# One of layer 1's two modulation sums goes from VectorE, ScalarE and GpSimd to TensorE, and from the first out projection into the layer 0 mixers

## The chip, the cores and the metric

The kernel runs on one core of one Trainium2 chip. The metric is device time in microseconds (us) of one execution; lower is better. An engine's instructions run in the order of its queue: PE is TensorE (weight loads apart, as PEld), DVE is VectorE, ACT is ScalarE, POOL is GpSimd, SP is the queue that issues all the DMAs.

## The reference

Two layers of a diffusion backbone over 640 tokens (128 of context, 512 latent) of width 2048. Each layer's norm is modulated by three vectors of 2048, for each of two conditions (`c_ctx` and `c`):

```
def adaln(x, cond, norm_w, w_ada, b_ada):
    mod = jax.nn.silu(cond) @ w_ada + b_ada
    shift, scale, gate = jnp.split(mod, 3, axis=-1)
    return rmsnorm(x, norm_w) * (1 + scale) + shift, gate
...
    for li in range(DEPTH):
        hc, gate_c = adaln(xc, cc, norm_w[li], w_ada[li], b_ada[li])
        hl, gate_l = adaln(xl, cl, norm_w[li], w_ada[li], b_ada[li])
        ...  # even layer: DeltaNet and windowed attention; odd layer: GLA and neighbourhood attention
        xc = xc + gate_c * (oc @ w_out)
        xl = xl + gate_l * (ol @ w_out)
```

So layer 1's shift and scale are each a product of two condition vectors with a 2048 x 2048 part of `w_ada[1]` (16.8 MB in float32). They depend on no token. They are needed when layer 1's input is normed, which is after the first out projection (`@ w_out` of layer 0).

## The kernel before

Activations stand transposed, 128 features by 640 tokens a tile (16 tiles). A projection is done in units: one unit makes 128 output features of all tokens, in two halves of 320 tokens, each an accumulator `acc` in PSUM (the pool `pacc` holds three). Weights come in quarters of a unit (`weights`, L1040 on): a DMA into `w_st`, ACT rounds it to `w_hi`, DVE subtracts to get `w_lo` (L1050); each of `w_st`, `w_hi`, `w_lo` has three buffers. For each of the 16 feature tiles and each half there are three matmuls (`hh,w_hi`, `hl,w_hi`, `hh,w_lo`), so a unit has 96 matmuls and a quarter 24.

The program has these stages: a start with layer 0's norm; the layer 0 mixers, where `run` lays the heads' streams and, as filling, the units of the input projection one after another on PE; the first out projection (`out_proj`); the layer 1 mixers; the second out projection. In the mixers of layer 0 the order of PE is that of the recording (`keep_in_program_order`), and so is it in `out_proj`; the other engines' order is set by a scheduler that works on modelled times.

There are two ways to make a modulation vector.

- `ada` gives it to TensorE. A step loads 128 x 512 of `w_ada` into a slot of `adv` (L1269), four matmuls of 32 columns each, on four column groups of the array, multiply it with the conditions (`ada_ps`; the profile counts two instructions for each, as they are float32), and DVE adds the PSUM tile to `adv` (L1286, or L1284 for the first of a chunk). 16 steps make a chunk of 512 outputs, 64 steps a vector. After a chunk `ada_out` transposes it and writes `mod`. Layer 0's gate is made this way in the layer 0 mixers, with one slot; its pacing is `yield 7`.
- `ada_vec` sums on vector engines. A step loads 128 x 512 of `w_ada` (L1305) and for each condition multiplies it with 128 scalars and adds it to a running 128 x 512 sum: on DVE in one instruction (L1319; L1317 for the first of a chunk), or on ACT (L1322, into `scale_t`) with the addition on POOL (L1324). After 16 steps PE sums over the partitions (`adv_ps`), and `ada_out` writes `mod`.

Before the change both vectors of layer 1 are made in `out_proj` of layer 0 with `ada_vec`: the scale (tile `scale`) with one condition on DVE and one on ACT and POOL, the shift (tile `vec`) with both on DVE. `side` advances both together. `out_proj` takes a step of this filling after every six of its main steps, and a main step is three matmuls; so 18 steps (16 and two more, a chunk) go with 324 matmuls, and the 72 steps with 1296.

When a unit is done, `residual` does three instructions on DVE (L1518: `x` from `acc`, gate and the old `x`; only then is `acc` free), a DMA writes `x` out, ACT squares it, POOL adds the square to `n_acc` (L1462), and when the scale of this tile is there POOL multiplies `x` with it (`scaled`, L1422, two instructions). Before, tiles wait for their chunk of the scale.

Of the kernel before, what the change touches and what calls it, by code (L numbers as in the profile page):

```python
# [1201 lines left out]
def run(g, main, *streams):  # L1202


    live = [[s, None, g.now] for s in streams]
    while live:
        for e in live:
            if e[2] <= g.now if e[1] is None else e[1]():
                try:
                    y = next(e[0])  # L1210
                    e[1], e[2] = (y, 0) if callable(y) else (None, g.now + (y or 0))
                except StopIteration:
                    live.remove(e)
                break
        else:
            if not main.step():
                nn = min([e[2] for e in live if e[1] is None] + [main.when()])
                assert nn < INF
                g.now = nn
# [147 lines left out]
def vec_store(pool, n, nt, width=512, name="vec"):  # L1367

    t = pool.tile([128, 2 + n, width], F32, name=name)
    return t[:, 0:2], [t[:, 2 + i] for i in range(n)], partial(pool.tile, [128, width], F32, name=f"{name}_t", bufs=nt)  # L1370


def ada_store(pool, n, k, width=512):

    w = width // 4
    t = pool.tile([128, w + n * k * width], F32, name="adv")
    return t[:, 0:w], [t[:, w + j * k * width:w + (j + 1) * k * width] for j in range(n)]
# [169 lines left out]
def body(nc, tc, I, O):  # L1547
    off = [(k, v.shape[1]) for k, v in const_table().items()]
    with ExitStack() as es:
        g = G()  # L1550
# [4 lines left out]
        pool = lambda e, n, b=1, **k: e.enter_context(tc.tile_pool(name=n, bufs=b, **k))  # L1555
# [34 lines left out]
        with ExitStack() as e1:  # L1590
            px = pool(e1, "px0")
# [12 lines left out]
            store = ada_store(px, 3, 4)  # L1604
# [45 lines left out]
        with ExitStack() as e1:  # L1650
            g.pt = pool(e1, "pt", 3)
            g.pz = pool(e1, "pz")
            g.pat = pool(e1, "pat")
            g.pss = pool(e1, "pss", 2, space=PSUM)
            g.psg = pool(e1, "psg1", 2, space=PSUM)
            a_setup(g, e1)
            b_setup(g, e1)
            g.spare = 8
            main = Main(g, hh, hl, zip(EARLY, parts), slabs[-1][0])
            get = lambda n, prio, now=False: main.ask(W[n], prio, now, n)  # L1660
            prepped, inverted, values, gates, queried, bgates, st = {}, {}, {}, {}, {}, {}, dict(b=0, joined=-1, scanned=-1, ready={}, gates=False)

            tri = g.pe.tile([128, T], F32, name="g_tri", tag="a_o1", bufs=2)
            nc.sync.dma_start(tri[:, 0:512], I["a_tab"])

            def first():
                ps = yield from get(32, -1)
                gs = g.pe.tile([128, T], F32, name="gs", tag="a_o0", bufs=2)
                for i in range(2):
                    nc.scalar.copy(gs[0:64, i * 320:i * 320 + 320], ps[i][0:64])  # L1670
                yield LAT["drain"]
                yield from a_gates(g, gs, tri)
                st["gates"] = True

            def prep():
                for h in range(8):
                    yield lambda: st["joined"] >= h - 2
                    k = a_conv(g, h, 1, (yield from get(8 + h, 0.5)))
                    yield lambda: st["scanned"] >= h - 2
                    q = a_conv(g, h, 0, (yield from get(h, 0.5)))  # L1680
                    yield LAT["conv"]
                    yield lambda: st["gates"]
                    prepped[h] = yield from a_prep(g, h, q, k)
                    st["ready"][h] = g.now

            def value():
                for h in range(8):
                    yield lambda: st["joined"] >= h - 1 and h in st["ready"]
                    values[h] = a_conv(g, h, 2, (yield from get(16 + h, 1)))
                    yield LAT["conv"]  # L1690
                    values[h, 1] = True

            def zgate():
                for h in range(8):
                    yield lambda: st["scanned"] >= h - 1 and len(st["ready"]) >= h + 1
                    gates[h] = silu2(g, (yield from get(24 + h, 2)), g.pz, "zs_a")

            def inverses():
                for h in range(8):
                    yield lambda: st["joined"] >= h - 1 and h in prepped  # L1700
                    yield max(0, st["ready"][h] + LAT["inv"] - LAT["invld"] - g.now)
                    inverted[h] = a_inverted(g, h, *prepped[h]["inv"]), g.now

            def scans():
                for h in range(8):
                    yield lambda: (h, 1) in values and h in inverted
                    yield max(0, inverted[h][1] + LAT["invld"] - g.now)
                    prepped[h]["inv"] = inverted.pop(h)[0]
                    oT = yield from a_scan(g, prepped.pop(h), values.pop(h), gates, st)
                    g.outs.emit(h, oT)  # L1710
                    st["scanned"] = h

            def queries():
                for h in range(8):
                    yield lambda: len(st["ready"]) >= h and st["b"] >= h - 1
                    if h == 0:
                        yield from b_kv(g, 0, get(41, 3), get(43, 3))
                    queried[h] = yield from b_query(g, h, get(33 + h, 3))
                    st["q", h] = g.now

            def bgate():
                for h in range(8):
                    yield lambda: h in queried and st["b"] >= h - 1
                    bgates[h] = silu2(g, (yield from get(45 + h, 4)), g.pz, bufs=2)

            def bs():
                for h in range(8):
                    if h == 4:
                        yield from b_kv(g, 1, get(42, 0), get(44, 0))
                    yield lambda: h in queried  # L1730
                    yield max(0, st["q", h] + LAT["rope"] - g.now)
                    yield from b_head(g, h, queried[h], bgates)
                    st["b"] = h + 1

            gate = ada(g, 0, (2,), [512] * (2048 // 512), ada_store(g.pa1, 1, 1, 512), 7)
            outs = g.outs = Outs(g, main, 53, I["w_out_even"], ORDER0, 2)
            run(g, main, inverses(), scans(), first(), prep(), value(), bs(), queries(), zgate(), bgate(), gate, outs.stream())
        e0.close()

        with ExitStack() as e1:  # L1740
            px = pool(e1, "px1")
            g.pt2 = pool(e1, "pt2")
            g.psg = pool(e1, "psg2", 4, space=PSUM)
            steps = ada_vec(g, 1, 1, vec_store(px, 4, 2, name="scale"), ('dve', 'act'))
            steps = side(steps, ada_vec(g, 1, 0, vec_store(px, 4, 2), ('dve', 'dve')))
            sh = mod(g, 1, 0)

            def end(t, xs, accs):

                cs = slice(t * 320, t * 320 + 320)  # L1750
                for _ in range(2):
                    yield
                R = yield from rstd(g, px, accs, t * 320, 320, 64)
                for k in range(16):
                    h = px.tile([128, T], F32, name="h_t", tag="h_t", bufs=3)
                    times(g, h[:, cs], xs[k][:, cs], R, k % 3)
                    for c0, c1, cd in REG:
                        c0, c1 = max(c0, cs.start), min(c1, cs.stop)
                        if c0 < c1:
                            hi, lo = (x[k][:, c0:c1] for x in (outs.main.hh, outs.main.hl))  # L1760
                            nc.scalar.activation(hi, h[:, c0:c1], AF.Identity, bias=sh[:, k, cd:cd + 1])
                            nc.vector.scalar_tensor_tensor(out=lo, in0=h[:, c0:c1], scalar=sh[:, k, cd:cd + 1], in1=hi,
                                                           op0=ALU.add, op1=ALU.subtract)
                    if k % 2:
                        yield

            out_proj(g, 0, outs, px, lambda n: I["xT"][n], lambda n: x1[n], steps,
                     lambda n: g.mod[1, 1][:, n] if g.mods.get((1, 1), 0) > n else None, end)
            hs = [(outs.main.hh[k], outs.main.hl[k]) for k in range(16)]
            hh, hl = zip(*hs)  # L1770

# [201 lines left out]
```

## Time and profile before

| | us |
|---|---|
| median of 3 runs (2791.26 to 2799.9) | 2797.22 |
| the profiled execution | 2803.32 |
| its span in the profile | 2801.5 |
| PE busy (share of the span) | 2623.7 (94%) |
| DVE busy | 1650.0 (59%) |
| ACT busy | 998.2 (36%) |
| POOL busy | 800.3 (29%) |

A busy time is the time in which at least one instruction of the engine ran. Matmuls are pipelined, so a busy PE need not be at its peak. What a change in one stage is worth has to be read from that stage. The granted clock tells TensorE's share of 2.4 GHz; 0.5 is 1.2 GHz.

### The profile page before, as it was taken

The page shows a single profiled execution, that of the slowest core. Times are in us where ns is not written, and L with a number is a line of the kernel's source. Part 1 is how long each engine was busy: PE and PEld are TensorE (multiplying, and loading weights), DVE is VectorE, ACT ScalarE, POOL GpSimd, SP SyncE. Part 2 cuts the span into 40 slices and gives each one's busy share as a digit, 9 for nine tenths or more (in the row PEclk, how much of TensorE's full clock was granted, in tenths as well). Part 3 has the DMA queues.
Part 4 walks back from the last instruction along what each step waited for, and adds up shares of the span by engine and source line. Part 5 has one row for each costly group of instructions (what it writes and reads, how often), then busy time and mean ns, then how long its engine had stood idle before and what let it go on. Part 6 is the DMA issues. An engine that isn't in the chain of part 4 may idle for free.

```text
span 2801.5 us, 53986 instructions
## 1 busy us (share of the span) xinstructions
PE 2623.7 (94%) x20855; PEld 2458.3 (88%) x20855; DVE 1650.0 (59%) x3618; ACT 998.2 (36%) x2214; POOL 800.3 (29%) x946
## 2 busy tenths in 40 slices
PE   6889899999999999997979899999999999999997
PEld 5778787787878988997879799999999999999996
DVE  5765556565655664469998855454553636455225
ACT  3232342333333434353333543334324333343222
POOL 2326415053350550005554431013001201220223
PEclk9989999999999999998889999999999999999998
DMA  9933333332322222247665332232332323225334
GB/s 330 304 91 92 92 92 86 95 95 81 103 85 72 76 69 69 79 162 233 216 205 169 117 101 91 80 112 70 103 110 75 98 78 103 97 66 178 99 99 136
DMA packets 264705, 329.81 MB, mean 118 GB/s; under 512 B 76013, under 2 KB 148925, under 8 KB 264447
## 3 DMA queue, kind: packets, MB, share of 16 engines
q1 hardware_dynamic: 264447, 326.35, 36.8%
q8 instruction: 164, 2.69, 0.4%
q14 instruction: 94, 0.77, 0.1%
HBM read 294.95 MB, written 28.68 MB: 116 GB/s over the span
## 4 chain that ended last, share of the span: by engine, by line
PE 70%; DVE 10%; issue 9%; DMA 7%; POOL 2%; ACT 1%; SPq 1%; DVEq 0%; POOLq 0%; ACTq 0%
PE acc L77 55%; PE a_st L77 3%; DVE vec L1319 2%; DMA a_df<-gc_d 2%; PE at_s L77 2%; PE at_o L77 2%; DVE w_lo L1050 1%; PE ada_ps L77 1%; DVE scale L1319 1%; PE c_ops L77 1%; PE at_pt L84 1%; DMA adv<-w_ada 1%; PE c_lv L77 1%; POOL i_tmp L493 1%; POOL i_S L495 1%
## 5 line engine op out<-in xcount | busy, mean ns | idle before, releaser
L77 PE MATMUL acc<-hh,w_hi 128*128 128x320 f32 (+1 forms) x4544 | 1462.7, 323 | 53.4 <-DVE x L1518 42.5
L77 PE MATMUL acc<-hl,w_hi 128*128 128x320 f32 (+1 forms) x4544 | 1425.9, 314 | 9.1 <-DVE hl L1228 8.5
L77 PE MATMUL acc<-hh,w_lo 128*128 128x320 f32 x4480 | 1405.3, 314 | 11.5 <-DVE w_lo L1050 11.5
L77 PEld LDWEIGHTS acc<-hh,w_hi 128*128 128x128 f32 (+1 forms) x4544 | 866.2, 191 | 101.6 <-issue 73.5
L77 PEld LDWEIGHTS acc<-hl,w_hi 128*128 128x128 f32 (+1 forms) x4544 | 866.9, 191 | 14.7 <-DVE hl L1228 12.2
L77 PEld LDWEIGHTS acc<-hh,w_lo 128*128 128x128 f32 x4480 | 856.9, 191 | 14.4 <-DVE w_lo L1050 13.5
L1050 DVE TENSOR_TENSOR w_lo<-w_st,w_hi 128x512 fp32r<-128x512 f32 x561 | 435.9, 778 | 537.3 <-ACT w_hi L1048 532.0
L1048 ACT CAST w_hi<-w_st 128x512 fp32r<-128x512 f32 (+1 forms) x604 | 364.8, 604 | 835.8 <-PE acc L77 713.2
L1319 DVE SCALAR_TENSOR_TENSOR vec<-vec,cond 128x256 f32<-128x256 f32 (+1 forms) x360 | 248.8, 727 | 22.3 <-DMA vec<-w_ada 21.1
L495 POOL TENSOR_TENSOR i_S<-i_S,i_tmp 40x30 f32<-40x30 f32 (+14 forms) x240 | 144.6, 602 | 18.6
L493 POOL TENSOR_TENSOR i_tmp<-i_S 40x30 f32<-40x30 f32 (+14 forms) x240 | 136.6, 569 | 18.1
L1324 POOL TENSOR_TENSOR scale<-scale,scale_t 128x512 f32<-128x512 f32 x60 | 94.5, 1575 | 121.5 <-ACT scale_t L1322 61.7
L928 POOL TENSOR_TENSOR c_X<-c_b 128x320 f32<-128x320 f32 x56 | 46.9, 837 | 227.0 <-PE c_lv L77 199.6
L1462 POOL TENSOR_TENSOR n_acc<-n_acc,n_sq 128x640 f32<-128x640 f32 (+1 forms) x30 | 47.8, 1595 | 204.0 <-ACT n_sq L1461 204.0
L302 POOL TENSOR_TENSOR a_at<-a_df,consts 128x640 f32<-128x640 f32 x8 | 13.0, 1627 | 323.8 <-PE a_st L77 97.2
L789 POOL TENSOR_TENSOR d_bias<-d_braw,d_mask 128x256 f32<-128x256 f32 x32 | 28.5, 920 | 230.6 <-PE tm_ps L84 90.7
L77 PE MATMUL ada_ps<-adv,cond 128*32 128x128 f32 x1536 | 68.1, 299 | 25.2 <-DMA adv<-w_ada 23.6
L215 DVE SCALAR_TENSOR_TENSOR a_y<-a_pad,consts,a_y 128x644 f32<-128x644 f32 x96 | 90.1, 938 | 2.1
L77 PEld LDWEIGHTS ada_ps<-adv,cond 128*32 128x32 f32 x1536 | 39.2, 116 | 46.1 <-DVE n_acc L1462 19.6
L1322 ACT ACTIVATE scale_t<-scale,cond 128x512 f32<-128x512 f32 x60 | 43.0, 722 | 95.7 <-DMA scale<-w_ada 83.8
L1050 POOL TENSOR_TENSOR w_lo<-w_st,w_hi 128x256 fp32r<-128x256 f32 (+1 forms) x43 | 35.8, 838 | 105.2 <-ACT w_hi L1048 82.7
L593 ACT ACTIVATE at_S<-at_S,at_nm 128x384 f32<-128x384 f32 (+2 forms) x80 | 47.5, 594 | 49.9 <-DVE at_nm L591 49.6
(321 smaller groups left out, 2894.1 us busy)
## 6 DMA issues: line engine op xcount, KB each, us to landing
w_st<-w_in_odd SPq DMA_DIRECT2D x232, 256.0 KB
adv<-w_ada SPq DMA_DIRECT2D x192, 256.0 KB
w_st<-w_in_even SPq DMA_DIRECT2D x188, 256.0 KB
w_st<-w_out_even SPq DMA_DIRECT2D x72, 256.0 KB
w_st<-w_out_odd SPq DMA_DIRECT2D x72, 256.0 KB
scale<-w_ada SPq DMA_DIRECT2D x64, 256.0 KB
vec<-w_ada SPq DMA_DIRECT2D x64, 256.0 KB
vec<-w_ada SPq DMA_DIRECT2D x128, 128.0 KB
```

Of the source, the lines that this page charges most:

```text
L77: i = self.nc.tensor.matmul(out, lhsT=lhsT, rhs=rhs, **kw)
L215: nc.vector.scalar_tensor_tensor(out=y, in0=pad[:, j:j + CL], scalar=w[:, j:j + 1], in1=y, op0=ALU.mult, op1=ALU.add)
L493: E.tensor_tensor(out=t, in0=S[:, j + 1:, j].unsqueeze(2).to_broadcast([40, n, j]), in1=S[:, j, 0:j].unsqueeze(1).to_broadcast([40, n, j]) ...
L495: E.tensor_tensor(out=S[:, j + 1:, 0:j], in0=S[:, j + 1:, 0:j], in1=t, op=ALU.add)
L593: nc.scalar.activation(S[:, 0:n], S[:, 0:n], AF.Exp, bias=nm, accum_out=den[:, 0:1])
L928: nc.gpsimd.tensor_tensor(out=pv(X[0])[:, :, 1 - d], in0=bv[:, :, 1 - d], in1=bm, op=ALU.subtract)
L1048: nc.scalar.copy(hi, st)
L1050: (nc.gpsimd if g.spare >= 0 else nc.vector).tensor_tensor(out=lo, in0=st, in1=hi, op=ALU.subtract)
L1319: nc.vector.scalar_tensor_tensor(out=acc[:, c], in0=st, scalar=sc, in1=acc[:, c], op0=ALU.mult, op1=ALU.add)
L1322: nc.scalar.activation(t, st, AF.Copy, scale=sc)
L1324: nc.gpsimd.tensor_tensor(out=acc[:, c], in0=acc[:, c], in1=t, op=ALU.add)
L1462: eng.tensor_add(accs[0][:, cs], accs[0][:, cs], t[:, cs])
```

## The change

Layer 1's scale is made by `ada` in the layer 0 mixers, with a pool of its own of three slots (`pv`), from the time that two heads are prepared, paced by `yield 4`. In `out_proj` only the shift is left, as it was, both conditions on DVE. `scaled` finds the scale there from the first tile on. The pool takes its place in SBUF from the scratch that the program holds for DMAs issued by GpSimd (`dynamic_dma_scratch_size`); no DMA of this kernel is issued there.

```diff
@@ -1651,6 +1651,7 @@
             g.pat = pool(e1, "pat")
+            g.pv = pool(e1, "pv")
             g.pss = pool(e1, "pss", 2, space=PSUM)
@@ -1733,16 +1734,21 @@
             gate = ada(g, 0, (2,), [512] * (2048 // 512), ada_store(g.pa1, 1, 1, 512), 7)
+            store = ada_store(g.pv, 3, 1)
+
+            def ahead():
+
+                yield lambda: len(st["ready"]) >= 2
+                yield from ada(g, 1, (1,), [512] * 4, store, 4)
+
             outs = g.outs = Outs(g, main, 53, I["w_out_even"], ORDER0, 2)
-            run(g, main, inverses(), scans(), first(), prep(), value(), bs(), queries(), zgate(), bgate(), gate, outs.stream())
+            run(g, main, inverses(), scans(), first(), prep(), value(), bs(), queries(), zgate(), bgate(), gate, ahead(), outs.stream())
...
-            steps = ada_vec(g, 1, 1, vec_store(px, 4, 2, name="scale"), ('dve', 'act'))
-            steps = side(steps, ada_vec(g, 1, 0, vec_store(px, 4, 2), ('dve', 'dve')))
             sh = mod(g, 1, 0)
...
-            out_proj(g, 0, outs, px, lambda n: I["xT"][n], lambda n: x1[n], steps,
-                     lambda n: g.mod[1, 1][:, n] if g.mods.get((1, 1), 0) > n else None, end)
+            out_proj(g, 0, outs, px, lambda n: I["xT"][n], lambda n: x1[n],
+                     ada_vec(g, 1, 0, vec_store(px, 4, 2), ("dve", "dve")),
+                     lambda n: g.mod[1, 1][:, n], end)
@@ -1960,7 +1967,7 @@
-    nc = _bacc.Bacc("TRN2", target_bir_lowering=False, num_devices=1)
+    nc = _bacc.Bacc("TRN2", target_bir_lowering=False, num_devices=1, dynamic_dma_scratch_size=1024)
```

Counted over the whole program, this takes 64 multiply-adds and 4 copies from DVE, 64 instructions from ACT, 60 additions from POOL, and 36 small matmuls from PE in the out projection; it puts 256 matmuls (512 instructions) and 4 transposes on PE and 64 additions or copies of 128 x 128 on DVE in the mixers. The 64 loads of 256 KB go from the one stage to the other. All other instructions stay in number, and PE's matmuls of the projections in the out projection stand as they did.

The change moves rows on DVE and on PE. First DVE in the first out projection, from one weight quarter within a unit to the next unit's residual (`vec` is the sum of the shift, `scale` that of the scale, `w_lo` the low part of a weight quarter). Before:

```order
L1050 TENSOR_TENSOR w_lo<-w_st,w_hi 128x512
L1319 SCALAR_TENSOR_TENSOR scale<-scale,cond 128x512
L1319 SCALAR_TENSOR_TENSOR vec<-vec,cond 128x512 x2
L1050 TENSOR_TENSOR w_lo<-w_st,w_hi 128x512
L1319 SCALAR_TENSOR_TENSOR scale<-scale,cond 128x512
L1319 SCALAR_TENSOR_TENSOR vec<-vec,cond 128x512 x2
L1319 SCALAR_TENSOR_TENSOR scale<-scale,cond 128x512
L1050 TENSOR_TENSOR w_lo<-w_st,w_hi 128x512
L1319 SCALAR_TENSOR_TENSOR vec<-vec,cond 128x512
L1518 SCALAR_TENSOR_TENSOR x_15722<-acc,mod_3936,x_old 128x128
```

And now, at a like place in a unit:

```order
L1050 TENSOR_TENSOR w_lo<-w_st,w_hi 128x512
L1319 SCALAR_TENSOR_TENSOR vec<-vec,cond 128x512 x3
L1050 TENSOR_TENSOR w_lo<-w_st,w_hi 128x512
L1319 SCALAR_TENSOR_TENSOR vec<-vec,cond 128x512 x4
L1050 TENSOR_TENSOR w_lo<-w_st,w_hi 128x512
L1319 SCALAR_TENSOR_TENSOR vec<-vec,cond 128x512 x4
L1050 TENSOR_TENSOR w_lo<-w_st,w_hi 128x512
L1319 SCALAR_TENSOR_TENSOR vec<-vec,cond 128x512 x2
L1518 SCALAR_TENSOR_TENSOR x_16062<-acc,mod_3955,x_old 128x128
L1518 SCALAR_TENSOR_TENSOR x_16062<-acc,mod_3955,x_old 128x192
```

The rows of `scale` are gone, and the scheduler has closed the gap with rows of `vec`: three or four sums stand between two weight quarters, as before, until the chunk's 32 are done. Then comes a stretch without sums, round a chunk's end:

```order
L1050 TENSOR_TENSOR w_lo<-w_st,w_hi 128x512
L1319 SCALAR_TENSOR_TENSOR vec<-vec,cond 128x512 x3
L1050 TENSOR_TENSOR w_lo<-w_st,w_hi 128x512 x2
L1518 SCALAR_TENSOR_TENSOR x_16211<-acc,mod_3955,x_old 128x128
L1518 SCALAR_TENSOR_TENSOR x_16211<-acc,mod_3955,x_old 128x192
L1518 SCALAR_TENSOR_TENSOR x_16211<-acc,mod_3955,x_old 128x320
L1050 TENSOR_TENSOR w_lo<-w_st,w_hi 128x512 x4
L1335 COPY vec<-adv_ps 128x128
```

Six weight quarters stand here with no sum between them.

Second, PE in the layer 0 mixers, soon after the second head is prepared (`a_st` is a step of a DeltaNet scan, `ada_ps` a step of a modulation sum). Before:

```order
L77 MATMUL acc<-hh_321,w_hi 128x320
L77 MATMUL acc<-hl_322,w_hi 128x320
L77 MATMUL acc<-hh_321,w_lo 128x320
L77 MATMUL acc<-hh_327,w_hi 128x320
L77 MATMUL acc<-hl_328,w_hi 128x320
L77 MATMUL acc<-hh_327,w_lo 128x320
L77 MATMUL a_st<-a_s_3264,a_wT 64x128 x2
```

Now:

```order
L77 MATMUL acc<-hh_321,w_hi 128x320
L77 MATMUL acc<-hl_322,w_hi 128x320
L77 MATMUL acc<-hh_321,w_lo 128x320
L77 MATMUL ada_ps<-adv,cond 32x128 x4
L77 MATMUL a_st<-a_s_3268,a_wT 64x128 x2
L77 MATMUL a_st<-a_s_3268,a_o_2150 64x128 x2
L77 MATMUL acc<-hh_327,w_hi 128x320
```

A step of the scale's sum stands between two matmuls of a projection unit; the projection's matmuls behind it are the same ones, later by that step. On SP the 64 loads (`adv<-w_ada`) stand among the mixers' own loads, each behind the matmuls that free its slot.

## Rows read from the trace of the kernel before

**Rows 1.** The page's 40 slices of the span, busy tenths of DVE.

```profile
DVE  5765556565655664469998855454553636455225
```

**Rows 2.** Windows: stretch, us, busy of PE, PEld, DVE, ACT, POOL, clock, DMA, GB/s.

```profile
600.00:800.00 200.00, 191.37 (x1750) 166.14 (x1749) 115.04 (x284) 71.64 (x176) 55.15 (x85) 0.97 0.32 94
...
1252.00:1520.00 268.00, 220.35 (x1439) 215.18 (x1437) 258.01 (x303) 84.86 (x132) 143.12 (x96) 0.89 0.66 214
...
2650.00:2700.00 50.00, 50.00 (x343) 50.00 (x342) 13.94 (x24) 11.38 (x18) 11.76 (x12) 1.00 0.31 101
```

**Rows 3.** Waits of PE from 1240 to 1600 us: total, times, longest.

```profile
PE acc L77 <- DVE x L1518: 42.5, 12, 8.0
PE acc L77 <- DVE w_lo L1050: 9.1, 6, 5.2
```

**Rows 4.** Groups on DVE, 1254 to 1520 us: busy us, mean ns, idle before.

```profile
L1319 DVE SCALAR_TENSOR_TENSOR vec<-vec,cond 128x512 f32<-128x512 f32 x120 | 135.2, 1147 | 0.1
L1319 DVE SCALAR_TENSOR_TENSOR scale<-scale,cond 128x512 f32<-128x512 f32 x60 | 63.9, 1065 | 0.6 <-DMA scale<-w_ada 0.6
L1050 DVE TENSOR_TENSOR w_lo<-w_st,w_hi 128x512 fp32r<-128x512 f32 x53 | 49.1, 926 | 3.5 <-ACT w_hi L1048 3.5
L1518 DVE SCALAR_TENSOR_TENSOR x<-acc,mod,x_old 128x320 f32<-128x320 f32 x13 | 7.0, 538 | 0.0
...
L1518 DVE SCALAR_TENSOR_TENSOR x<-acc,mod,x_old 128x192 f32<-128x192 f32 x13 | 5.2, 402 | 0.0
L1518 DVE SCALAR_TENSOR_TENSOR x<-acc,mod,x_old 128x128 f32<-128x128 f32 x13 | 4.4, 339 | 0.0
```

**Rows 5.** Groups on POOL, 1260 to 1500 us.

```profile
L1324 POOL TENSOR_TENSOR scale<-scale,scale_t 128x512 f32<-128x512 f32 x56 | 88.7, 1585 | 70.3 <-ACT scale_t L1322 57.3 <-ACT scale L1322 11.4
L1462 POOL TENSOR_TENSOR n_acc<-n_acc,n_sq 128x640 f32<-128x640 f32 x11 | 20.1, 1825 | 29.4 <-ACT n_sq L1461 29.4
```

**Rows 6.** Timeline, 1400 to 1425 us: start, us, engine, line, instruction.

```profile
1401.02 1.75 DVE L1319 SCALAR_TENSOR_TENSOR scale<-scale,cond 128x512 f32<-128x512 f32 x1
...
1402.69 1.75 DVE L1319 SCALAR_TENSOR_TENSOR vec<-vec,cond 128x512 f32<-128x512 f32 x1
...
1409.67 0.74 DVE L1319 SCALAR_TENSOR_TENSOR vec<-vec,cond 128x512 f32<-128x512 f32 x1
...
1410.34 0.74 DVE L1319 SCALAR_TENSOR_TENSOR scale<-scale,cond 128x512 f32<-128x512 f32 x1
```

**Rows 7.** Timeline of PE round a step of layer 0's gate, 612.9 to 616 us.

```profile
613.43 0.31 PE L77 MATMUL acc<-hh,w_lo 128*128 128x320 f32 x1
613.67 0.42 PE L77 MATMUL ada_ps<-adv,cond 128*32 128x128 f32 x8
614.03 0.42 PE L77 MATMUL acc<-hh,w_hi 128*128 128x320 f32 x1
...
614.28 0.31 PE L77 MATMUL acc<-hl,w_hi 128*128 128x320 f32 x1
```

**Rows 8.** The tile ada_ps, 235 to 1000 us (the sum: 235 to 840 us).

```profile
L77 PE MATMUL ada_ps<-adv,cond x464: 272/296/421, 238.5 to 831.0; 128*32 128x128 f32 x155
L1286 DVE TENSOR_TENSOR adv<-adv,ada_ps x55: 272/286/290, 239.0 to 831.3; 128x128 f32<-128x128 f32 x55
...
sum 605.00, PE 24.94 PEld 9.20 DVE 16.45; mean PE 6.23 PEld 2.30 DVE 4.11
```

**Rows 9.** Waits of the SP queue, 260 to 840 us: total, times, longest.

```profile
SPq L1269 <- PE ada_ps L77: 62.9, 33, 4.2
```

**Rows 10.** Groups on DVE and POOL in the second out projection, 2600 to 2700 us.

```profile
L1050 DVE TENSOR_TENSOR w_lo<-w_st,w_hi 128x512 fp32r<-128x512 f32 x29 | 20.8, 716 | 61.3 <-ACT w_hi L1048 61.3
...
L1462 POOL TENSOR_TENSOR n_acc<-n_acc,n_sq 128x640 f32<-128x640 f32 x7 | 11.1, 1580 | 78.1 <-ACT n_sq L1461 78.1
L1422 POOL TENSOR_TENSOR x<-x,consts 128x512 f32<-128x512 f32 x7 | 7.3, 1041 | 0.0
L1422 POOL TENSOR_TENSOR x<-x,consts 128x128 f32<-128x128 f32 x7 | 2.8, 401 | 0.0
```

## The prediction

> **What bounds the kernel now.** I read the page's slices first: DVE, at five or six tenths elsewhere, stands at eight and nine for five slices from 1260 us on [rows 1]. That is the first out projection. Then windows, for the stages that the change touches [rows 2]. In the mixers of layer 0 PE is busy for 191 of 200 us and DVE for 115: PE sets the pace. From 1252 to 1520 us, the stretch in which both sums are made, DVE is busy for 258 of 268 us, PE for 220 at a mean clock of 0.89, POOL for 143. So here DVE sets the pace. The waits say so from the other side: in and round this stretch PE waited 42.5 us for the residuals that free `acc`, in 12 waits, and 9.1 us for `w_lo` [rows 3]. What this stretch would be with a light DVE is seen in the second out projection, which does the same matmuls without a filling: 343 of them in 50 us, clock 1.00, DVE under a third busy [rows 2]. That is 0.146 us a matmul.
>
> So one stage has DVE too full and PE to spare, and the change takes DVE work out of it; the other has PE full, and the change puts PE work into it. The answer is a difference of two terms.
>
> **Term 1, the out projection.** The 72 filling steps go with 1296 matmuls of `acc`, before and after. At 0.146 us these are 189 us. The shift's own 72 small matmuls stay; at 0.05 us each (eight in 0.42 us [rows 7]) they add 4. PE's floor is 193 us, against 268 now: at most 75 us are to be had.
>
> What can DVE do? Its price depends on POOL. Two sums with POOL running start 1.67 us apart (1401.02 and 1402.69), two without it 0.67 (1409.67 and 1410.34), each 0.07 to 0.08 less than its duration [rows 6]. Means of 1147 and 1065 ns [rows 4] lie between. I take 0.075 us off every duration.
>
> - At today's prices the scale goes with 60 x (1.065 - 0.075) = 59 us and some 2 for its firsts and copies, and 197 of the 258 stay.
> - At the price without POOL, what stays is 120 x 0.67 = 80 for the shift, 5 for its firsts and copies, 53 x (0.716 - 0.075) = 34 for `w_lo` (the price of the second out projection [rows 10]), and 13 x (0.538 + 0.402 + 0.339 - 0.225) = 14 for the residuals: 133.
> - POOL does not go to nothing. The scale's additions, the largest thing on it, go [rows 5]; squares and scaling stay, 1.580 + 1.041 + 0.401 = 3.02 us a unit [rows 10], 41 us for 13.5 units in place of 143. Today's excess is 258 - 133 - 42 (the scale at 0.67) = 83 us of DVE for 143 of POOL, 0.58 each. So 41 us of POOL cost 24, and DVE needs 157 us.
>
> 157 is under PE's 193, so PE becomes the bound on average. In the Trainium skill, SBUF — State Buffer, section Who interferes with whom, an instruction of DVE with two inputs in SBUF and a GpSimd one that reads SBUF take turns on a shared port for a whole instruction. By that rule the sums fall to 0.67 us wherever POOL is idle; if they kept today's mean, DVE's 197 would be the floor in place of PE's 193. The two rows at 1.67 and 0.67 agree with the rule.
>
> An average isn't all. The order on DVE keeps three or four sums between two weight quarters until a chunk's sums are done, then none for some six quarters. In such a dense quarter DVE needs 4 x 0.67 + 0.64 + 0.26 (a quarter of a residual) + 0.44 (24 us of POOL's hindrance over 54 quarters) = 4.0 us, and PE 24 x 0.146 = 3.5. DVE falls back by 0.5 us a quarter, over 8 quarters a chunk and four chunks 17 us. `w_lo` has three buffers, so most of this lag is hidden there; `acc` has three for two a unit, so a late residual is not, and that is the wait that rows 3 show to be the large one. I take 12 of the 17. The stretch is then 193 + 12 = 205 us: **63 us less**. Its ends: 75, if all lag is hidden; 42, if POOL holds up DVE for all its 41 us (0.84 us a quarter, 27 in all) and the clock is 0.97, as in the mixers, in place of 1.00 (6 us), which gives 226.
>
> ACT loses 64 instructions and the loads of the scale leave SP; neither is a bound here (ACT 85 of 268 us, DMA 0.66). The scaling of `x` by POOL now follows at once; nobody waits for it before the stage's end.
>
> **Term 2, the mixers.** Layer 0's gate shows the new step already, 58 times between 235 and 840 us [rows 8]. One step seen: a matmul of `acc` starts at 613.43, the next but one at 614.28, with the step's eight instructions between [rows 7]. Two matmuls alone would take 0.29, so a step costs 0.56 us of PE. 64 steps: 36 us, and 1 us for four transposes: **37 us more**. This is on the path, as PE is busy for 191 of 200 us there and a projection unit always stands ready to fill a wait, so a step put into a wait only pushes that unit out.
>
> Ends: by busy time a step is 24.94 / 58 = 0.43 us, 27.5 for 64, which holds if the gaps at its two sides shrink. The difference is where a rule of the Trainium skill speaks against this change: TensorEngine Tiling (Array Packing), section Key Properties, says that a change of tiling mode drains TensorE, and each step changes to four column groups and back. By the rule the sum is 36, by busy time alone 27.5. The step that I measured (0.24 us from the matmul before to the step's start, where 0.146 is usual) agrees with the rule.
>
> At the other end, DVE adds a PSUM tile of 286 ns for each step [rows 8], 18 us. DVE has 85 of 200 us free there, so I cost this at nothing; all on the path would make 55 us. The 64 loads (16.8 MB) meet DMA engines at 0.32, hence nothing either. Each load stands on SP behind the matmul that frees its slot, and the mixers' loads behind it wait too; that is a rival below.
>
> **The sum**: -63 + 37 = -26 us on the profiled execution's 2803.3, 0.93%. The median of the runs is 0.2% lower, 2797.2; less 26 it is **2771 us**.
>
> **The rivals.**
> - *PE paces all and the step costs its busy time only.* For it: 157 against 193 leaves DVE slack, and `w_lo` has buffers. Against it: the dense quarters, and the 0.56 us. -75 + 27.5 = -47: 2750 us.
> - *The dense quarters keep DVE the bound.* The lag of 0.84 us a quarter and the clock of 0.97: -42 + 39 = -3: 2794 us, no change that can be told. For it: the order is as dense as before in those quarters, and PE's 42.5 us of waits came from just such lags. Against it: POOL falls to under a third.
> - *Slower: SP holds the mixers' loads.* SP waited 62.9 us for the gate's matmuls in 33 waits, 1.9 us each [rows 9]. 64 more loads are 122 us of waiting on SP, with weight quarters and the scans' small loads queued behind, and PE waits for those. If 0.55 us a load reaches PE, the mixers cost 72 and the sum is +9: 2806 us. It turns slower by more than 0.3% from 71 us, that is 1.1 us a step. Against it: the gate's steps do this now, and PE has 9 us in 200 without work.
>
> **How the numbers follow.** The forecast's case (gain 53 to 70, cost 33 to 42: 2760 to 2786 us) has 0.56; PE pacing all 0.13; DVE still the bound 0.19; SP 0.12. About 0.3% (8.4 us) is what a measurement of this kernel can tell from no change. Faster: 0.56 + 0.13 + 0.03 of the third, 0.72; the same: 0.16 + 0.02, 0.18; slower 0.10. The range is 2752 to 2802 us: it leaves out the fast end of the second case and most of the fourth.
>
> **What would show it.** In the changed profile the stretch with `vec` sums in the out projection should last about 205 us, with PE's clock above 0.95, the sums' mean near 0.85 us in place of 1.15, and PE's wait for residuals at 8 to 15 us. In the mixers the last attention step should come some 37 us later than now, with 122 steps of `ada_ps` and PE still at 19 of 20 us. The prediction is wrong if the out projection's waits stay near 40 us though POOL is light, if PE in the mixers shows new waits for loads or for DVE's `adv`, or if steps cost well under 0.5 us.

## The result, and the profile after

The changed kernel takes 2764.02 us (median of 4 runs, 2759.45 to 2772.63) beside 2798.56 for the kernel before: a ratio of 0.9879, 95% interval 0.9862 to 0.9896, so 34.5 us less. Run again later, with other runs of the kernel before beside it, it took 2761.36 against 2799.48 (0.9867, 0.9846 to 0.9888): 38.1 less. The forecast was 2771.

The page's 40 slices of the changed kernel, busy tenths of DVE and the granted clock; the five slices at eight and nine of [rows 1], from the nineteenth on, are now at six to eight, and the clock has no dip there:

```profile
DVE  5765556564655565448786845455553645555225
...
PEclk9989999999999999999999999999999999999998
```

In the kernel before, the first three of these slices have the clock at eight:

```profile
PEclk9989999999999999998889999999999999999998
```

Windows of the changed kernel: a stretch of the mixers, and the stretch of the out projection in which the shift is summed (columns as in [rows 2]: us, then busy time of PE, PEld, DVE, ACT, POOL, then clock, DMA share, GB/s):

```profile
600.00:800.00 200.00, 192.39 (x1768) 165.36 (x1768) 117.22 (x283) 69.06 (x177) 56.74 (x88) 0.96 0.37 111
1277.00:1481.00 204.00, 201.39 (x1412) 198.66 (x1411) 155.47 (x236) 45.37 (x71) 44.68 (x39) 1.00 0.61 197
```

In the out projection PE is now busy for 201 of 204 us at a clock of 1.00, DVE for 155. The bound has changed hands. The waits of PE from 1262 to 1570 us, where [rows 3] had 42.5 and 9.1:

```profile
PE acc L77 <- DVE w_lo L1050: 3.9, 5, 2.2
PE acc L77 <- DVE x L1518: 2.6, 3, 1.2
...
PE acc L77 <- ACT w_hi L1048: 2.2, 4, 1.1
```

And DVE's groups there (1277 to 1480 us), which answer to the first and third of [rows 4]:

```profile
L1319 DVE SCALAR_TENSOR_TENSOR vec<-vec,cond 128x512 f32<-128x512 f32 x120 | 96.6, 846 | 1.8 <-DMA vec<-w_ada 1.4
L1050 DVE TENSOR_TENSOR w_lo<-w_st,w_hi 128x512 fp32r<-128x512 f32 x56 | 43.6, 782 | 29.0 <-ACT w_hi L1048 28.9
```

The same 120 sums took 135.2 us before. They are the same instructions; POOL beside them went from 143 us busy (of 268) to 45 (of 204).

To compare stages I take three marks on PE: the first matmul `gc_ps` (the gates at the mixers' start), the last `at_o` of layer 0, and the first `n_ss` (the norm that ends the out projection). The groups of these tiles, changed kernel (the times at the end are the first and last start):

```profile
L77 PE MATMUL gc_ps<-g_or,g_tri x8: 274/275/303, 182.3 to 183.5; 128*128 128x40 f32 x4, 128*128 128x80 f32 x4
...
L77 PE MATMUL at_o<-at_P,b_v x96: 270/275/377, 1154.2 to 1274.0; 128*128 128x128 f32 x96
...
L77 PE MATMUL n_ss<-consts,n_acc x40: 197/197/218, 1495.8 to 1513.3; 128*64 128x1 f32 x40
```

and the kernel before:

```profile
L77 PE MATMUL gc_ps<-g_or,g_tri x8: 274/275/303, 186.9 to 188.1; 128*128 128x40 f32 x4, 128*128 128x80 f32 x4
...
L77 PE MATMUL at_o<-at_P,b_v x90: 270/275/421, 1151.1 to 1249.1; 128*128 128x128 f32 x90
...
L77 PE MATMUL n_ss<-consts,n_acc x40: 197/197/218, 1541.6 to 1559.1; 128*64 128x1 f32 x40
```

The mixers went from 1062.2 to 1091.7 us, the out projection from 292.5 to 221.8. The differences of the same marks in every profile of this study, in us:

| kernel | mixers | out projection | device time, median |
|---|---|---|---|
| before | 1062.2 | 292.5 | 2797 to 2799 |
| changed | 1091.7 | 221.8 | 2764.0 |
| changed, again | 1092.1 | 222.5 | 2761.4 |
| e1_both | 1094.7 | 292.6 | 2826.8 |
| e2_nosum | 1058.4 | 225.5 | 2728.6 |
| e3_pool | 1092.9 | 265.7 | 2807.5 |
| e5_dve | 1057.0 | 275.6 | 2777.0 |
| e4_twos | 1089.2 | 221.6 | 2758.6 |
| e6_scratch | 1058.5 | 295.2 | 2798.3 |
| e7_dvemix | 1095.5 | 220.7 | 2790.1 |
| e8_shift | 1141.5 | 214.0 | 2802.9 |
| e9_fours | 1088.2 | 222.7 | 2751.1 |
| e10_both4 | 1062.5 | 222.8 | 2729.5 |

One profile of the mixers is good to some 3 us: four kernels without the moved sum (before, e2, e5, e6) lie between 1057.0 and 1062.2, mean 1059.0, and four with it in the changed kernel's form (changed, again, e1, e3) between 1091.7 and 1094.7, mean 1092.9. So the moved sum costs the mixers 34 us. It is work and not waiting: between the two marks PE was busy for 1006.7 us before and for 1034.1 in the changed kernel, and idle for 55.5 and 57.6. The start, up to the first mark, is 181 to 187 us in all but e7, whatever the change; that the changed kernel's was 5 us shorter than before's in the first two profiles is no effect of it.

### The profile page after: what moved, and what is told of

The parts are those of the page before. It is cut to its first block, busy times and chain, and to the rows that moved or that the text cites. A ratio compares the mean times of both kernels' runs of the same rounds, so it can differ in the third digit from the quotient of the medians.

```text
span 2757.7 us, 54675 instructions
## 1 busy us (share of the span) xinstructions
PE 2624.2 (95%) x21303; PEld 2444.2 (89%) x21303; DVE 1558.3 (57%) x3614; ACT 956.0 (35%) x2150; POOL 696.0 (25%) x886
## 5 line engine op out<-in xcount | busy, mean ns | idle before, releaser
L77 PEld LDWEIGHTS acc<-hh,w_hi 128*128 128x128 f32 (+1 forms) x4544 | 857.0, 189 | 67.3 <-issue 41.0
L77 PEld LDWEIGHTS acc<-hl,w_hi 128*128 128x128 f32 (+1 forms) x4544 | 858.1, 189 | 13.0 <-DVE hl L1228 11.4
L1050 DVE TENSOR_TENSOR w_lo<-w_st,w_hi 128x512 fp32r<-128x512 f32 x561 | 426.7, 762 | 574.5 <-ACT w_hi L1048 565.5
L1319 DVE SCALAR_TENSOR_TENSOR vec<-vec,cond 128x256 f32<-128x256 f32 (+1 forms) x360 | 213.1, 636 | 24.6 <-DMA vec<-w_ada 22.8
L77 PE MATMUL ada_ps<-adv,cond 128*32 128x128 f32 x2048 | 93.0, 293 | 33.4 <-DMA adv<-w_ada 24.3
L77 PEld LDWEIGHTS ada_ps<-adv,cond 128*32 128x32 f32 x2048 | 49.0, 113 | 63.9 <-DVE n_acc L1462 20.1
L1286 DVE TENSOR_TENSOR adv<-adv,ada_ps 128x128 f32<-128x128 f32 x144 | 40.5, 284 | 71.7 <-PE ada_ps L77 70.4
L614 ACT COPY at_P<-at_pt 128x384 f32<-128x384 f32 (+2 forms) x80 | 36.6, 457 | 72.0 <-PE at_pt L84 71.9
```

The costliest lines, as they stand in the source:

```text
L77: i = self.nc.tensor.matmul(out, lhsT=lhsT, rhs=rhs, **kw)
L614: nc.scalar.copy(P[:, 0:nb], pt[:, 0:nb])
L1050: (nc.gpsimd if g.spare >= 0 else nc.vector).tensor_tensor(out=lo, in0=st, in1=hi, op=ALU.subtract)
L1286: nc.vector.tensor_add(acc, acc, ps)
L1319: nc.vector.scalar_tensor_tensor(out=acc[:, c], in0=st, scalar=sc, in1=acc[:, c], op0=ALU.mult, op1=ALU.add)
```

## The experiments

The theory: the out projection gained because POOL's additions no longer hold up DVE, and because DVE has 64 sums fewer, so that PE became its bound; the mixers lost a fixed price for each step of the sum. The rivals: that the number of DVE's instructions alone matters; that steps sit free in waits of PE; that the loads on SP hold up the mixers.

**e1_both: the mixers' term alone.** The kernel before, with the same sum made in the mixers too, into a vector of its own.

```diff
+    spare = g.spared and (l, part) == (1, 1)
+    mc = mod(g, 9 if spare else l, part)[:, n0:n0 + nt]
...
-            run(g, main, inverses(), ..., bgate(), gate, outs.stream())
+            run(g, main, inverses(), ..., bgate(), gate, ahead(), outs.stream())
```

> The kernel before, with the scale's sum made a second time by TensorE in the layer 0 mixers, into a vector that nobody reads; the out projection keeps both sums on the vector engines. It measures the mixers' term by itself. By the prediction's price (0.56 us of PE a step) the time rises by 36 to 37 us over before, all of it before the last attention step of layer 0. In the changed kernel that point came only 25 us later, so a second theory: part of the steps sit in waits of PE and the cost is 25 us or less. A third (the loads hold up SP) would give over 50.

Measured: 2826.77 against 2799.0 (ratio 1.0098, 1.0082 to 1.0115), 28 us more, with an interval of 23 to 32; its out projection is that of before, 292.6 us. The mixers' mark says 34, and the changed kernel stands 33 to 35 us over the next one. So the price lies between 28 and 35 us: somewhat less than 37, and far from the 50 of the third theory. By this time alone the 25 us of the second theory can't be excluded; the marks, 34 us in four kernels, speak against it.

**e2_nosum: the out projection's term alone.** The changed kernel without `ahead()`; layer 1's scale is its bias alone, and the sum is left out.

> The changed kernel without the scale's sum (left out: layer 1's scale is its bias alone). It measures the out projection's term by itself. By the trace of the changed kernel, where the stretch from the last attention step to the norm shrank from 292 to 222 us, the time falls by some 70 us under before, to about 2728; by the prediction's 63, to 2735. If the changed kernel had gained elsewhere (its start was 5 us earlier), it falls by less than 65, and the rest shows outside the out projection.

Measured: 2728.62 (ratio 0.9744, 0.973 to 0.9759), 70.4 us under before, as the marks of the changed kernel had said; its own marks put 67 of it in the out projection. Its stretch with sums:

```profile
1249.00:1450.00 201.00, 197.05 (x1375) 194.61 (x1374) 152.39 (x231) 43.06 (x67) 43.50 (x38) 0.99 0.60 193
```

PE 197 of 201 us, as in the changed kernel: the gain needs nothing of what happens in the mixers.

**e3_pool: POOL's additions put back, without the sum.** The changed kernel with 60 additions on two private tiles of POOL, advanced with the shift's sum.

```diff
+            def idle():
+                for i in range(60):
+                    nc.gpsimd.tensor_tensor(out=pa, in0=pa, in1=pb, op=ALU.add)
+                    yield
...
-                     ada_vec(g, 1, 0, vec_store(px, 4, 2), ("dve", "dve")),
+                     side(ada_vec(g, 1, 0, vec_store(px, 4, 2), ("dve", "dve")), idle()),
```

> The changed kernel with 60 more additions on POOL of 128x512 in the out projection, on two tiles that nobody else touches, so that POOL is as busy there as before while DVE's instructions stay those of the changed kernel. Theory of the shared access (0.58 us of DVE for each us of POOL): 95 us of POOL cost DVE 55, DVE needs 155 + 55 = 210 us against PE's 193, the sums' mean goes from 0.85 to over 1.05 us, and the time is 15 to 25 us over the changed kernel. Rival, that the gain came from the number of DVE instructions alone: no more than 3 us, and the mean stays 0.85.

Measured: 2807.48 (ratio 1.0033, 1.002 to 1.0045): 43 us over the changed kernel, and over the kernel before. No instruction reads what these additions write. Windows of it, while the 60 additions run (1276.9 to 1420.5) and after them, and groups on DVE and POOL over both:

```profile
1278.00:1421.00 143.00, 116.03 (x728) 113.15 (x727) 125.81 (x122) 23.13 (x36) 113.48 (x78) 0.88 0.46 146
1421.00:1525.00 104.00, 100.12 (x690) 98.37 (x689) 76.11 (x115) 22.57 (x35) 24.91 (x22) 0.98 0.57 182
```

```profile
L1319 DVE SCALAR_TENSOR_TENSOR vec<-vec,cond 128x512 f32<-128x512 f32 x120 | 129.8, 1123 | 0.7 <-DMA vec<-w_ada 0.2
L1050 DVE TENSOR_TENSOR w_lo<-w_st,w_hi 128x512 fp32r<-128x512 f32 x57 | 54.8, 964 | 30.7 <-ACT w_hi L1048 30.7
...
L1760 POOL TENSOR_TENSOR idle_a<-idle_a,idle_b 128x512 f32<-128x512 f32 x60 | 93.7, 1561 | 3.8
```

The mean of the same 120 sums is back at 1123 ns, and `w_lo` at 964. DVE needs 202 us in place of 155: 47 us for 94 us of POOL, 0.50 each (0.58 was worked out from the trace before). That half of the theory held, and the rival with the number of instructions fell. PE stopped for DVE and not for POOL; its waits from 1235 to 1620 us, where the changed kernel had 2.6 and 7.0 us:

```profile
PE acc L77 <- DVE x L1518: 25.0, 7, 6.8
PE acc L77 <- DVE w_lo L1050: 9.6, 8, 4.6
```

The time rose by twice what I expected. I had spread the cost evenly, but POOL ran its 60 additions in 144 us, where PE was busy for 116 of 143 us at a clock of 0.88, and PE was nearly full in the time after them, 100 of 104 us. That this uneven spread is the whole of the difference I did not test.

**e5_dve: POOL out of it, more on DVE.** The kernel before, with the scale's second condition on DVE.

```diff
-            steps = ada_vec(g, 1, 1, vec_store(px, 4, 2, name="scale"), ('dve', 'act'))
+            steps = ada_vec(g, 1, 1, vec_store(px, 4, 2, name="scale"), ('dve', 'dve'))
```

> The kernel before, with the scale's second condition on DVE too, in place of ACT and POOL: 64 more instructions on DVE, 60 fewer on POOL, nothing in the mixers. Shared access: DVE gains 64 x 0.67 = 43 us of work and is spared 95 x 0.58 = 55, so the time is 5 to 15 us under before and the sums' mean falls to 0.85 us. Number of DVE instructions alone: 64 x 1.07 = 68 us more on the engine that sets the pace there, so some 60 us over before.

Measured: 2776.98 (ratio 0.9922, 0.9908 to 0.9936), 22 us under before with 64 DVE instructions more. Window and groups of its out projection (groups 1245 to 1500 us):

```profile
1245.00:1500.00 255.00, 217.18 (x1476) 210.92 (x1475) 244.33 (x372) 44.63 (x71) 57.91 (x40) 0.91 0.69 224
```

```profile
L1319 DVE SCALAR_TENSOR_TENSOR scale<-scale,cond 128x512 f32<-128x512 f32 x120 | 99.5, 851 | 0.1
L1319 DVE SCALAR_TENSOR_TENSOR vec<-vec,cond 128x512 f32<-128x512 f32 x120 | 96.8, 823 | 0.0
```

DVE does 372 instructions in less time than 303 before, and is still the bound (244 of 255 us, clock 0.91). So by the marks 17 of the out projection's 71 us came back by taking ACT's and POOL's part out and paying for it on DVE (22 by the times); the other 54 need the sum gone. ACT's 64 multiplications went too, which no run separates here; e3 put back POOL's additions alone.

**e8_shift: the other sum too.** The shift by TensorE in the mixers, after the scale.

```diff
                 yield from ada(g, 1, (1,), [512] * 4, store, 4)
+                yield from ada(g, 1, (0,), [512] * 4, store, 4)
...
-                     ada_vec(g, 1, 0, vec_store(px, 4, 2), ("dve", "dve")),
+                     (),
```

> The changed kernel with the shift made by TensorE in the layer 0 mixers too, after the scale; the out projection has no sums left. PE is the bound of the out projection in the changed kernel, with under 10 us of waits and 4 of small matmuls, so there is little more to gain there: 5 to 12 us less, against 64 more steps at 0.5 to 0.56 us, 32 to 36 more: 20 to 30 us over the changed kernel.

Measured: 2802.93 (ratio 1.0019, 1.001 to 1.0028), 39 us over the changed kernel. Its out projection, from the last attention step to the norm:

```profile
1323.00:1537.00 214.00, 214.00 (x1462) 214.00 (x1462) 69.42 (x114) 52.65 (x83) 42.06 (x44) 1.00 0.37 122
```

PE is busy for every us of it, with nothing to wait for: this is the floor (without the shift's own small matmuls, which the prediction put at 4 us), and the changed kernel is 8 us over it. There was 8 us to gain, and the mixers paid 50 for it, more than my 36. Between the marks of the mixers PE was busy for 1072.0 us, 38 more than in the changed kernel, about as priced, and idle for 69.5, which is 12 more. So the excess is idle time of PE; no single wait of PE there grew by more than 3 us, and what causes it is open.

**e7_dvemix: the scale in the mixers on DVE.**

```diff
-            store = ada_store(g.pv, 3, 1)
+            store = vec_store(g.pv, 3, 1)
...
-                yield from ada(g, 1, (1,), [512] * 4, store, 4)
+                yield from ada_vec(g, 1, 1, store, ('dve', 'dve'), 9)
```

> The changed kernel with the scale's sum in the layer 0 mixers on DVE (64 steps of two sums of 128x512, paced 9 apart) in place of TensorE. PE is spared 33 us or so of steps; DVE gets 128 x 0.67 to 1.0 = 86 to 128 us where it has some 400 of 1000 free. If DVE's free time there hides it, 25 to 33 us under the changed kernel, about 2735. Rival: a sum of 0.7 to 1.7 us in front of a scan's short instructions on DVE makes PE wait in its fixed order; half a us for each of the 64 steps takes it all back, and the time is that of the changed kernel or above.

Measured: 2790.12 (ratio 0.9972, 0.9961 to 0.9984), 26 us over the changed kernel: the rival's time came. The mixers are as long as with TensorE's steps (1095.5 us), though PE has none of them to do, and the start is longer by some 25 (the first `gc_ps` at 207.0 us). Two waits of PE (185 to 1260 us) that stood at 1.6 and 1.0 us in the kernel before, and DVE's timeline shortly ahead of that `gc_ps`:

```profile
PE gc_ps L77 <- DVE g_or L168: 16.9, 1, 16.9
PE a_ops L84 <- ACT a_oraw L456: 8.7, 1, 8.7
```

```profile
195.79 0.88 DVE L215 SCALAR_TENSOR_TENSOR a_y<-a_pad,consts,a_y 128x644 f32<-128x644 f32 x1
196.59 0.19 DVE L154 TENSOR_SCALAR gs<-gs 128x80 f32<-128x80 f32 x1
...
196.76 1.40 DVE L1319 SCALAR_TENSOR_TENSOR vec<-vec,cond 128x512 f32<-128x512 f32 x2
```

The scheduler put sums of 0.7 us between the gates' instructions of 0.2 us, which make a chain; that is the 25 us of the start. In the mixers PE was idle for 81 us between the marks, against 53 to 56 in the four kernels without the moved sum, and busy for some 10 more. Which instructions of DVE are behind that, beside the 8.7 us above, I did not trace. At least in the start, free time on an engine was not room, because what ran there were short links of a chain.

**e6_scratch: the smaller scratch alone**, on the kernel before.

> The kernel before with the smaller scratch alone. No DMA is issued by GpSimd, so no change (under 3 us). If the 5 us by which the changed kernel's start was shorter in its profile come from the smaller scratch, they show here.

Measured: 2798.29 (ratio 1.0004, 0.9995 to 1.0013): nothing.

**e4_twos, e9_fours, e10_both4: what a step costs.** In the trace of the changed kernel most steps stand alone, and ten pairs stand together. I worked out the cost of each group as in [rows 7], where it lies between matmuls of a projection: from the matmul ahead to the second one behind, less two matmuls. The median is 0.552 us for a group of 8 instructions (49 such) and 0.772 for one of 16 (5 such). So 8 instructions more cost 0.22 us, and each of these groups costs 0.33 whatever its length.

```diff
e4: store = ada_store(g.pv, 2, 2); ... [512] * 4, store, 8)
e9: store = ada_store(g.pv, 1, 4); ... [512] * 4, store, 16)
e10: e9, and gate = ada(g, 0, (2,), [512] * (2048 // 512), ada_store(g.pa1, 1, 4, 512), 28)
```

> The changed kernel with two feature tiles in a step of the mixers' sum: 32 steps of 16 instructions, paced half as often, the same matmuls, half the changes between four column groups and the whole array, 32 fewer additions on DVE. If the 0.13 us between a step's cost (0.56) and its busy time (0.43) is paid at those changes, 32 x 0.13 = 4 us less than the changed kernel (2 to 8). If it is paid by each group of four matmuls, no change.

Measured: 2758.62 (ratio 0.9861, 0.9848 to 0.9873), 5 us under the changed kernel; the intervals of the two overlap, so alone this was a hint. The expected 4 us (2 to 8) are met all the same.

> The changed kernel with four feature tiles in a step of the scale's sum: 16 steps of 32 instructions with one slot of four tiles, paced 16 apart. In the traces so far a group of 8 instructions between two matmuls of a projection costs 0.552 us of PE and one of 16 costs 0.772, so a group costs 0.33 and each 8 instructions 0.22 more. Then 64 single steps cost 35 us, 32 double ones 25, and 16 of four 16 x 1.21 = 19 us: 14 to 16 us under the changed kernel, about 2749. If what a group costs is not fixed (or a whole slot of 1 MB comes too late from memory and PE waits for it), 5 us or less.

Measured: 2751.08 (ratio 0.9829, 0.9808 to 0.9851), 10 us under the changed kernel run beside it (2761.36), where 14 to 16 were expected; the two intervals overlap a little. By the marks the mixers are only 4 us shorter (1088.2): PE was busy for 9 to 11 us less there than in the two profiles of the changed kernel, and idle for 5 to 7 us more (62.8). The profile is of the slowest of its four executions. So this run supports a price for each group, but not its size.

> The kernel with four feature tiles a step, and layer 0's gate made so too (16 steps paced 28 apart in place of 64 paced 7 apart). The gate's 64 steps in the mixers cost 35 us by the same price and would cost 19: 28 to 32 us under the changed kernel, about 2734. If PE has waits in the mixers that the gate's short steps fill, less of it: 15 to 20.

> The changed kernel itself beside the two above on one chip, so that their distance to it is taken there: 2764, ratio 0.988 to the kernel before.

Measured: the changed kernel as expected, 2761.36 (0.9867), and e10_both4 2729.45 (ratio 0.975, 0.9733 to 0.9767), 32 us under the changed kernel beside it, and 70 under the kernel before. One of its groups on PE's timeline:

```profile
621.43 0.31 PE L77 MATMUL acc<-hh,w_lo 128*128 128x320 f32 x1
621.67 1.08 PE L77 MATMUL ada_ps<-adv,cond 128*32 128x128 f32 x32
622.68 0.41 PE L77 MATMUL acc<-hh,w_hi 128*128 128x320 f32 x1
622.93 0.31 PE L77 MATMUL acc<-hl,w_hi 128*128 128x320 f32 x1
```

From 621.43 to 622.93 are 1.50 us; less two matmuls, 1.21, as 0.33 + 4 x 0.22 has it. The changed kernel has 106 groups of 8 and 10 of 16 in the mixers, e10 has 32 of 32: by these prices 27 us less, and PE's busy time between the marks fell by 28 to 30 us, at the same idle time (56.3). Its mixers (1062.5 us) do two vectors in the time that the kernel before took for one.

## Why the prediction was right, and where its sizes were off

**Which engine sets the pace**: here the prediction held at every point. The out projection went over from DVE to PE: DVE at 155 us for a forecast of 157, the sums' mean at 846 ns for 0.85 us, the clock at 1.00. The split of DVE's price into its own time and POOL's hindrance, made from two pairs of rows, was the step that carried this, and e3 and e5 showed it from both sides. By the Trainium skill, SBUF — State Buffer, section Who interferes with whom, the two engines take turns on a shared port: the traces agree, at 0.50 us of DVE for each us of POOL in e3.

**Term 1 was mis-sized**: 63 us forecast, 71 measured. The part at fault is the 12 us for the dense quarters in which DVE falls back behind PE. The three waits above sum to 8.7 us over the whole of 1262 to 1570 us, and PE's wait for residuals among them, which I gave 8 to 15 us, is 2.6. From the shift's first load (1275.6) to its last transpose (1474.4) are 199 us: 6 over the floor of 193, where I had 12. The other 2 us lie in the kernel before, whose stretch is 269.5 us by the same two events, not 268. I let rows 3 speak for the new state, but they show a DVE that never catches up; in the new one DVE gets ahead, and waits 29.0 us for the next weight quarter (the row of `w_lo` above; 3.5 in [rows 4]). That it starts each dense stretch with its buffers full is my reading; no row shows it.

**Term 2 was slightly too high**: 37 us forecast, 34 by the marks, 28 to 35 by the times. The price of a step was right (0.56, then 0.552 measured). But ten pairs of steps stand together, and a pair costs 0.772 in place of 1.10, which is 3 us. The rule that a change of tiling mode drains TensorE (the Trainium skill, TensorEngine Tiling (Array Packing), section Key Properties) agrees with the groups of 8, 16 and 32 instructions, which share one price of 0.33 us a group; busy time alone, 0.43 a step, has no such share. Its sum of 27.5 us could not be told from e1's 28; the marks and the groups decide against it. Nor is the fixed price that of any group: in the changed kernel 2, 6 and 8 instructions of `at_o`, which use the whole array, cost 0.223, 0.671 and 0.893 us between the same matmuls by the same reading, 0.112 each and nothing fixed. So it belongs to the change to column groups and back.

**The rivals.** PE pacing all was right for the out projection and wrong for the step's price. DVE remaining the bound fell; its sum has a cost of 39 us for the mixers where 37 had been worked out, which the prediction does not explain. That SP would hold up the mixers began just as said: SP waited 127.1 us for the sums' matmuls, against [rows 9]'s 62.9:

```profile
SPq L1269 <- PE ada_ps L77: 127.1, 69, 5.7
```

but PE's busy time in the mixers stayed at 192 of 200 us, and its waits for loads hardly grew (for `adv` 2.2 us before, 2.1 and 3.0 in the two profiles of the changed kernel). The loads behind were early enough.

The sum by stages is -71 + 34 = -37 us, by the medians -34.5 and -38.1. Both errors went the same way, so that nothing cancelled, and the forecast of -26 was too small by a quarter to a third.

## What to carry to other kernels

Price an engine's instructions by what runs beside them: the additions that GpSimd took over here cost VectorE half a us for each us, and moving them, with ScalarE's part of the sum, onto VectorE itself was faster than leaving them where they were. When work on column groups is put among the matmuls of a full TensorE, count the groups and not the instructions: the matmuls of two sums in a quarter as many groups were worth almost as much again as the change itself. And look at what the engine with free time does there, since a chain of short instructions has no room for long ones.

## What the runs showed that I had not expected

Leaving projection matmuls for a group on four column groups and coming back costs 0.33 us, whatever the group's length (0.552, 0.772 and 1.21 us for 8, 16 and 32 instructions): two and a quarter matmuls of 320 columns. And 94 us of additions on POOL whose result nothing reads made the kernel 43 us slower, over half of it in stops of PE (35 us of waits for DVE, against 10), whose clock was 0.88 meanwhile.
